# Low parts of the keys' weights on one engine, and another place for the conformer's norm, in a hybrid attention, Hyena and conformer layer

## The chip, the cores and the metric

The kernel runs on one core of a Trainium2 chip. The core has engines with a queue of instructions each: TensorE (PE in the profile; PEld are its weight loads), VectorE (DVE), ScalarE (ACT), GpSimd (POOL) and SyncE (SP), which here only issues transfers; 16 DMA engines move the data. An engine works through its queue in order. The metric is the device time of one execution in microseconds (us); several timed runs are taken, and one more execution is recorded by the hardware profiler.

## The reference

One layer over 512 latent tokens of width 1024, arranged as 8 rows of 64, and 256 context tokens:

```
h  = modulate(rmsnorm(x), sh1, sc1);   hc = modulate(rmsnorm(ctx), csh1, csc1)
q, k, v, hy_in, cf_in = split(h @ w_in);   kc, vc = hc @ w_in[:, keys and values]
attn = softmax over (an 8 x 16 window of latents, and all context) in 8 heads of 64
hy   = two gated long convolutions of hy_in
y    = depthwise_conv31(a * sigmoid(g)) + b,          a, g = split(cf_in)   # 512 x 256
cf   = silu((y - mean(y)) * rsqrt(var(y) + eps) * ln_g + ln_b)              # over the 256 channels
x    = x + g1 * (concat(attn, hy, cf) @ w_out)
x    = x + g2 * expert_choice_moe(modulate(rmsnorm(x), sh2, sc2))           # 16 experts, 64 tokens each
out  = rmsnorm(x)
```

All inputs and the output are fp32. The last line of the conformer, from the mean to the silu, is the norm over channels of which the change speaks.

## The kernel before

**Exact products from two halves.** The projections run on TensorE in a rounded fp32 format. To keep precision each operand is split in a high part (a copy in the rounded format, on ACT, L515) and a low part (the rest, a subtraction, L516). A product is then three matmuls that add up in one PSUM bank (mm3, L547): high by high (L548), high by low (L549), low by high (L550). split (L510) treats a weight buffer of 128 x 2048 in four pieces of 512 columns. The table DVE_LO (L491) lists, for each weight buffer, the pieces whose subtraction goes to VectorE; the others go to GpSimd. The keys' weights are two buffers: ('k', 0) with the first half of the 1024 input channels and ('k', 1) with the second; each has two pieces in the table.

**Stages.** The Hyena, conformer, query and value parts of the projection come first, woven together by an order string (L823). Beside them runs conv_cf (L585), the 31-tap convolution: two channel tiles, 31 dependent steps on VectorE each (L587, L590), into the tiles yc. The values' projection ends with the context's values, ctx_v, whose second result is copied from PSUM by VectorE (L105, vc). The small products of the modulation, adaln(2), come about there too; their results are read from PSUM by VectorE at L459 (a bank of tag T) and L486 (a bank of tag Y).

Then `finish(ln_cf())` (L826) issues the whole norm. ln_cf (L595) is a generator of two steps. Step one: two matmuls with ones give the channel mean (L598), VectorE subtracts it (L601), ACT squares into two tiles sq (L603). Step two: 16 small matmuls sum the squares per token (L609), twelve tiny VectorE operations form the reciprocal root (rsqrt_mean, L144 to L154), a diagonal tile dg is filled (L614), a matmul spreads it (L616), VectorE multiplies (L618), ACT applies the silu (L619), and mix_store writes the result as high part (ACT, L561) and low part (VectorE, L562) into the tiles mixh and mixl of the output projection.

Behind it in the program come the splits of the two keys' weight buffers (L855), fetch_bias(0) (two transfers of the position bias into tiles g, issued by POOL, L841), build_tm(0) (a memset at L845 and six POOL subtractions from g, L849, three for each g), and fetch_bias(1), two more g.

Then the keys (L872 to L894): for each half u of the input channels, first the products for the context (tiles pC, four of 128 x 256, L884 by mm3), then those for the latents (pP, four of 128 x 512), 48 matmuls each. The context's banks are taken from the tags T and Y in turn (tiles 0 and 2 from T, 1 and 3 from Y), and all are held from u = 0 to the copies behind the products of u = 1 (L887, L889). The third bank user of the norm, like its first two (all psY, "pL"), is of tag Y as well.

Attention follows. On TensorE its order is written out (L1100): a score step S (L932), the output projection's first part x0 for one block of tokens (out_part, L903, four channel tiles: two of the Hyena, two of the conformer), a score step, a transposition T, and so on. build_tm(1) and fetch_bias(2) stand ahead of it (L1097). The experts come last: 384 transfers of 1 MB for their weights.

**Order and buffers.** Outside the stretches with a written order, a list scheduler in the compiler sets each engine's queue: it takes what is ready by its own estimate of times, the earliest in the program first. Tiles with the same tag share a fixed number of buffers: PSUM has tags A (4 banks), T (2) and Y (2); the big weight tiles share 24 buffers (U); the tiles named g, sq, dg, xo and some others (L98) share two buffers of the pool early. A tile's buffer is released when its last reader is done. The helpers used, free and pump (L61 to L82) count big buffers in program order and issue the next weight transfers while the count is low enough.

Of the kernel before, what the change touches and what calls it, by code (L numbers as in the profile page):

```python
# [50 lines left out]
def hybrid_kernel(ctx: ExitStack, tc: tile.TileContext, a, out: bass.AP):  # L51
# [13 lines left out]
    def U(name, dt=FT):  # L65
        used[0] += 1
        assert used[0] <= NU, name
        return big.tile([128, 2048], dt, name=name, tag="U")
# [11 lines left out]
    def free_only(k=1):  # L80
        used[0] -= k
# [7 lines left out]
    def psY(name="psY"):  # L89
        return psum.tile([128, 512], FT, name=name, tag="Y", bufs=2)  # L90

    def W(name="w", dt=FT):
        if name in ("g", "aff2", "lists", "od", "sn", "u", "xo", "sig", "sq", "dg", "arg", ):
            return early.tile([128, 512], dt, name=name, tag="w", bufs=2)
        return work.tile([128, 512], dt, name=name, tag="w")
# [4 lines left out]
    def copy(out_, in_):  # L100
        alt[0] ^= 1
        if alt[0]:
            nc.scalar.activation(out_, in_, AF.Copy)  # L103
        else:
            nc.vector.tensor_copy(out_, in_)  # L105
# [30 lines left out]
    def small_t(name, n, dt=FT, bufs=2):  # L136
        return work.tile([128, n], dt, name=name, tag=name, bufs=bufs)

    def rsqrt_mean(dst, ss, n, scale=1.0 / D):

        v = small_t("rv", n)
        t = small_t("rt", n)
        y = small_t("ry", n, I32)
        nc.vector.tensor_scalar(v, ss, scale, EPS, op0=OP.mult, op1=OP.add)  # L144
        nc.vector.tensor_scalar(y, v.bitcast(I32), -0.5, 1597463007.0, op0=OP.mult, op1=OP.add)
        nc.vector.tensor_scalar(v, v, -0.5, None, op0=OP.mult)
        yf = y.bitcast(FT)
        for i in range(3):
            if n == 1:
                nc.vector.scalar_tensor_tensor(t, yf, v, yf, op0=OP.mult, op1=OP.mult)  # L150
            else:
                nc.vector.tensor_mul(t, yf, yf)
                nc.vector.tensor_mul(t, t, v)
            nc.vector.scalar_tensor_tensor(dst if i == 2 else yf, t, 1.5, yf, op0=OP.add, op1=OP.mult)  # L154
# [11 lines left out]
    def take(key):  # L166
        while key not in ready:
            assert loads and used[0] < NU, key
            go = loads.popleft()
            if go is not None:  # L170
                go()
        return ready.pop(key)
# [315 lines left out]

    ADA_KEEP = [7, 4, 2, 0]
    KEEP = {'hy1': 8, 'hy0': 7, 'cf': 10, 'q': 8, 'v': 7}  # L490
    DVE_LO = {('q', 0): (0, 2), ('q', 1): (1, 3), ('k', 1): (0, 1), ('k', 0): (2, 3), ('cf', 1): (0, 1), ('hy0', 1): (2, 3), ('cf', 0): (1, 3), ('hy0', 0): (0, 2)}  # L491
    ADA = [(4, 0), (4, 4), (2, 8), (2, 10)]

    def modulate_split(src, n, v, name, pool="01010101"):
# [15 lines left out]
    def split(raw, keep, dve=()):  # L510
        hi = U("wh", FR)
        lo = U("wl", FR)
        for i in range(4):
            s = slice(i * 512, (i + 1) * 512)
            nc.scalar.activation(hi[:, s], raw[:, s], AF.Copy)  # L515
            (nc.vector if i in dve else nc.gpsimd).tensor_sub(lo[:, s], raw[:, s], hi[:, s].bitcast(FT))  # L516
        free(1, keep)
        return hi, lo
# [5 lines left out]
    def next_split():  # L524
        c, u = splits.popleft()
        presplit[c, u] = split(take(("win", c, u)), KEEP[c], DVE_LO.get((c, u), ()))

# [19 lines left out]
    def mm3(ps, l, r, start, stop):  # L547
        mm(ps, l[0], r[0], start=start, stop=False)  # L548
        mm(ps, l[0], r[1], start=False, stop=False)  # L549
        return mm(ps, l[1], r[0], start=False, stop=stop)  # L550
# [7 lines left out]
    def mix_store(i, k, src):  # L558

        h = cr(v512(mixh[i])[:, k])  # L560
        nc.scalar.activation(h, tr(src), AF.Copy)  # L561
        nc.vector.tensor_sub(cr(v512(mixl[i])[:, k]), tr(src), h.bitcast(FT))  # L562
# [32 lines left out]
    def ln_cf():  # L595
        ps = psY("pL")
        for i in range(2):
            mm(ps, ones, yc[i], start=(i == 0), stop=(i == 1))  # L598
        sq = []
        for i in range(2):  # L600
            nc.vector.tensor_sub(yc[i], yc[i], ps)  # L601
            sq.append(W("sq"))
            nc.scalar.activation(sq[i], yc[i], AF.Square)  # L603
        yield

        ps = psY("pL")
        for c in range(4):
            for i in range(2):
                mm(ps[:, c:c + 1], sq[i][:, 128 * c:128 * c + 128], one256, start=(i == 0), stop=(i == 1))  # L609
        rs = small_t("rsl", 4, bufs=1)  # L610
        rsqrt_mean(rs, ps[:, 0:4], 4, 1.0)
        dg = W("dg")
        for c in range(4):
            nc.vector.tensor_scalar(dg[:, 128 * c:128 * c + 128], ident, rs[:, c:c + 1], 256.0, op0=OP.mult, op1=OP.mult)  # L614
        ps = psY("pL")
        mm(ps, ones, dg, start=True, stop=True)  # L616
        for i in range(2):
            nc.vector.tensor_mul(yc[i], yc[i], ps)  # L618
            nc.scalar.activation(yc[i], yc[i], AF.Silu,  # L619
                                 scale=p1[:, P1["lg"].start + i:P1["lg"].start + i + 1],  # L620
                                 bias=p1[:, P1["lb"].start + i:P1["lb"].start + i + 1])
            mix_store(1, 2 + i, yc[i])
        free_only(1)
        yield
# [145 lines left out]
    def finish(*gens):  # L770
        for g in gens:
            for _ in g:
                pass
# [46 lines left out]
    with ExitStack() as ordered:  # L820
# [2 lines left out]
        for w in "......s.............h............hh.......m...hm..h...h....m..m..h...h..h...h...m....hh..........h.m...mm..hh...n.h.h....h..c....m..xcnh..n..hh..m....c....c..n..c.sxn.m....c.c.c........c..c..x..c.....cc.....c........cccccccccccc":  # L823
            next(side[w], None)
        finish(side["."], *[side[w] for w in "hmncx"])
    finish(ln_cf())  # L826
    vblk = lambda c: vv[:, c // 16] if c % 16 == 0 else vo[:, c // 16]


# [6 lines left out]
    def fetch_bias(hp):  # L836
        for s in range(2):
            rb[hp, s] = g = W("g")[:, 0:8 * RPBW]
            src = bass.AP(tensor=rp.tensor, offset=rp.offset + (2 * hp + s) * 15 * RPBW,
                          ap=[[1, 16], [RPBW, 8], [1, 7 * RPBW + 48]])  # L840
            nc.gpsimd.dma_start(g[:, 0:7 * RPBW + 48], src)  # L841
# [12 lines left out]
    for u in range(2):  # L854
        parts.append([t.rearrange("p (k n) -> p k n", n=512) for t in split(take(("win", "k", u)), 2, DVE_LO.get(("k", u), ()))])  # L855
    fetch_bias(0)
# [6 lines left out]
    def load_wo(n, u, keep):  # L863
        w = take(("wo", n, u))
        if u == 0:
            for k in range(4):
                nc.vector.tensor_mul(v512(w)[:, k], v512(w)[:, k], g1bc[:, n * 512:(n + 1) * 512])
        hi, lo = split(w, keep)
        wov[n, u] = (v512(hi), v512(lo))
# [5 lines left out]
    for u in range(2):  # L875
        hi, lo = parts[u]
        if u:
            KK.extend([U("KK") for _ in range(2)])
        for ctx_ in (True, False):
            for m in range(4):  # L880
                s = slice(m * 128, (m + 1) * 128)
                for k in range(4):
                    kg = 4 * u + k
                    mm3((psc if ctx_ else pss)[m], (hi[:, k, s], lo[:, k, s]),  # L884
                        (ch(kg), cl(kg)) if ctx_ else (hh(kg), hl(kg)), kg == 0, kg == 7)
                if u and ctx_:
                    copy(kat(m)[:, 512:768], psc[m])  # L887
                elif u:
                    copy(kat(m)[:, 0:512], pss[m])  # L889
            if u and ctx_:  # L890
                free_only(2)
                load_wo(0, 1, 2)
        if u == 0:
            free_only(2)  # L894
# [578 lines left out]
```

## Time and profile before

| | us |
|---|---|
| median of 3 timed runs | 1320.08 (1317.94 to 1324.70) |
| profiled execution | 1325.77 |
| its span, first to last instruction | 1324.0 |
| busy: PE, DVE, ACT, POOL | 1247.9, 512.2, 223.7, 155.2 |
| mean granted TensorE clock, share of 2.4 GHz | 0.988 |
| DMA over the span | 345 GB/s |

Stages in the profiled execution, in us from the start of the span: projections to 212.6; keys to 258.8; attention and output projection to about 360; routing to 388; experts to the end. All times below are on that scale. In the rows, `a<-b,c` says that tile a is written from b and c, `xN` that N instructions are merged, and a bracket gives the idle time of the engine before them with what ended it. Matmul ends are modelled, so starts are safer than durations.

### The profile page before, as it was taken

Reading aid. Unit: us, or ns where it says so; the run is one execution under the profiler, and the core shown is the slowest. Engines: PE = TensorE matmul, PEld = TensorE weight load, DVE = VectorE, ACT = ScalarE, POOL = GpSimd, SP = SyncE. Lnnn points to the kernel's source line nnn. Section 1 sums busy time; section 2 is a strip of 40 time slices with the busy share of each in tenths; the row PEclk is TensorE's granted clock in tenths of the full one; section 3 lists DMA queues with packets and bytes.
Section 4 is the critical chain, followed back from the end, with each engine's and each line's share of the span. In section 5 each row is a group of like instructions: output and inputs, shape, how many; then the busy total and the mean of one; then the engine's idle time right before and its main releaser. Section 6 shows DMA issues by size and latency. Waiting matters only on the chain.

```text
span 1324.0 us, 14793 instructions
## 1 busy us (share of the span) xinstructions
PE 1247.9 (94%) x5916; PEld 566.1 (43%) x5916; DVE 512.2 (39%) x1034; ACT 223.7 (17%) x480; POOL 155.2 (12%) x166
## 2 busy tenths in 40 slices
PE   5899988999889999999999999999999999999996
PEld 2577667866634333333333333333333333333332
DVE  6878998788570121222212123121211212121232
ACT  3542232345410010101101011010101001010111
POOL 1343443556210000000000000000000000000000
PEclk9999998999989999999999999999999999999999
DMA  9944026532488999999999999999999999999997
GB/s 349 382 170 187 21 68 180 206 110 96 148 362 355 419 420 419 420 419 419 420 420 419 420 419 420 420 419 420 419 420 420 419 420 419 420 420 420 419 419 296
DMA packets 72979, 457.99 MB, mean 346 GB/s; under 512 B 7364, under 2 KB 9228, under 8 KB 21710
## 3 DMA queue, kind: packets, MB, share of 16 engines
q1 hardware_dynamic: 71662, 453.64, 84.4%
q0 software_dynamic: 912, 3.06, 0.8%
q8 instruction: 46, 0.75, 0.2%
q10 hardware_dynamic: 336, 0.35, 0.1%
q14 instruction: 23, 0.19, 0.0%
HBM read 453.87 MB, written 2.36 MB: 345 GB/s over the span
## 4 chain that ended last, share of the span: by engine, by line
PE 50%; DMA 33%; DVE 13%; issue 2%; ACT 2%; POOL 0%; POOLq 0%; SPq 0%; ACTq 0%; DVEq 0%
DMA ld<-in_w_dram 32%; PE pa L1309 18%; PE py L1349 8%; DVE glu L590 4%; PE pZ L1202 3%; PE pG L1182 2%; PE pa L1310 1%; PE pP L550 1%; PE pP L549 1%; PE pP L548 1%; PE pX L548 1%; PE pS L932 1%; DMA out_dram<-acc 1%; PE pO L963 1%; PE pX L549 1%
## 5 line engine op out<-in xcount | busy, mean ns | idle before, releaser
L1310 PE MATMUL pa<-ld,xh 128*64 128x512 f32 x1024 | 465.0, 599 | 13.3 <-DMA ld<-in_w_dram 13.3
L1309 PE MATMUL pa<-ld,xh 128*64 128x512 f32 x1024 | 467.2, 599 | 0.2 <-DVE xh L1062 0.2
L1349 PE MATMUL py<-ld,xh 128*64 128x512 f32 x1024 | 224.8, 596 | 1.0 <-DMA ld<-in_w_dram 1.0
L1309 PEld LDWEIGHTS pa<-ld,xh 128*64 128x64 f32 x1024 | 132.2, 137 | 215.2 <-issue 207.0
L1205 DVE TENSOR_TENSOR acc<-acc,pZ 128x512 f32<-128x512 f32 x112 | 73.2, 685 | 286.3 <-PE pZ L1202 285.8
L1310 PEld LDWEIGHTS pa<-ld,xh 128*64 128x64 f32 x1024 | 132.7, 137 | 87.9 <-issue 56.6
L1349 PEld LDWEIGHTS py<-ld,xh 128*64 128x64 f32 x1024 | 72.2, 138 | 141.9 <-issue 136.6
L1377 POOL DMA_INDIRECT out_dram<-yg,rwA x1 | 1.1, 1112 | 931.2 <-DVE yg L1376 931.2
L1060 ACT ACTIVATE xh<-pT,B,A 128x64 f32<-128x64 f32 (+1 forms) x60 | 24.4, 406 | 447.8 <-PE pT L1190 337.1
L1353 DVE SCALAR_TENSOR_TENSOR yg<-py,rwA,g1bc 128x512 f32<-128x512 f32 x16 | 12.0, 751 | 211.5 <-PE py L1349 211.5
L1202 PE MATMUL pZ<-yg,oh 64*128 64x512 f32 x240 | 83.2, 640 | 3.0 <-DVE acc L1205 2.3
L516 POOL TENSOR_TENSOR wl<-ld,wh 128x512 fp32r<-128x512 f32 x44 | 65.0, 1506 | 79.2 <-ACT wh L515 60.5
L548 PE MATMUL pP<-hh,wh 128*128 128x512 f32 x144 | 58.3, 406 | 1.2 <-ACT hh L505 1.2
L549 PE MATMUL pP<-hl,wh 128*128 128x512 f32 x144 | 57.0, 397 | 1.5 <-DVE hl L507 1.5
L550 PE MATMUL pP<-hh,wl 128*128 128x512 f32 x144 | 56.4, 398 | 1.1 <-DVE wl L516 1.1
L590 DVE SCALAR_TENSOR_TENSOR glu<-glu,p 128x512 f32<-128x512 f32 x60 | 55.3, 922 | 1.2
L1336 PE MATMUL pT<-c,au 128*128 128x128 f32 x256 | 48.1, 316 | 6.2 <-DVE xh L1339 2.2
L1182 PE MATMUL pG<-ld,ohg 128*64 128x512 f32 x224 | 52.5, 592 | 0.0
L103 ACT ACTIVATE xg<-pG 128x512 f32<-128x512 f32 x7 | 4.2, 598 | 275.0 <-PE pG L1182 275.0
L1062 DVE TENSOR_SCALAR xh<-pT,A,B 128x64 f32<-128x64 f32 (+1 forms) x60 | 20.6, 344 | 76.1 <-ACT xh L1060 28.5
L1202 PEld LDWEIGHTS pZ<-yg,oh 64*128 64x128 f32 x240 | 22.1, 184 | 63.2 <-issue 37.3
L1336 PEld LDWEIGHTS pT<-c,au 128*128 128x128 f32 x256 | 36.1, 209 | 26.9 <-DVE acc L1205 12.5
(342 smaller groups left out, 1349.8 us busy)
## 6 DMA issues: line engine op xcount, KB each, us to landing
ld<-in_w_dram SPq DMA_DIRECT2D x384, 1024.0 KB, 19.9
ld<-in_w_mod_dram SPq DMA_DIRECT2D x24, 1024.0 KB, 14.7
ld<-in_w_in_dram SPq DMA_DIRECT2D x11, 1024.0 KB, 7.5
ld<-in_w_out_dram SPq DMA_DIRECT2D x4, 1024.0 KB, 11.9
ld<-in_x_dram SPq DMA_DIRECT2D x2, 1024.0 KB, 12.0
ld<-in_x_dram SPq DMA_DIRECT2D x4, 512.0 KB, 6.6
out_dram<-acc SPq DMA_DIRECT2D x4, 512.0 KB, 16.8
g<-in_rpb_dram POOLq DMA_DIRECT2D x8, 244.5 KB, 4.6
```

The lines of the kernel that those rows point to most:

```text
L516: (nc.vector if i in dve else nc.gpsimd).tensor_sub(lo[:, s], raw[:, s], hi[:, s].bitcast(FT))
L548: mm(ps, l[0], r[0], start=start, stop=False)
L549: mm(ps, l[0], r[1], start=False, stop=False)
L550: return mm(ps, l[1], r[0], start=False, stop=stop)
L590: nc.vector.scalar_tensor_tensor(yc[i], glt[i][:, j:j + 512], cw[:, i, j:j + 1], yc[i], op0=OP.mult, op1=OP.add)
L1182: mm(pg[64 * h:64 * h + 64], g[:, 64 * b:64 * b + 64], xblk(b)[:, 512 * h:512 * h + 512], start=(b == 0), stop=(b == 3))
L1202: mm(ps[h], oh[pr, 128 * c:128 * c + 128], yg[pr], start=True, stop=True)
L1205: nc.vector.tensor_add(ablk(c)[:, s], (ablk if e else xblk)(c)[:, s], ps[h])
L1309: mm(pa[f][0:64], xT[:, k, cs], w1[:, s], start=(k == 0), stop=(k == 7))
L1310: mm(pa[f][64:128], xT[:, k, cs], w3[:, s], start=(k == 0), stop=(k == 7))
L1336: nc.tensor.transpose(p[:, i * 128:(i + 1) * 128], au[f][:, c:c + 255:2], ident)
L1349: mm(py[64 * h:64 * h + 64], hT[:, f], w2[:, i * 1024 + 512 * h:i * 1024 + 512 * h + 512], start=(f == 0), stop=(f == 15))
```

## The change

Two things. The entries of the keys' weights leave the table, so that all eight low pieces are subtracted by GpSimd. And the norm is no longer issued whole ahead of the keys: the generator is kept, and one step of it is issued behind the latents' products of tile 2 in the first half of the input channels, the other behind those of tile 3.

```
-    DVE_LO = {('q', 0): (0, 2), ('q', 1): (1, 3), ('k', 1): (0, 1), ('k', 0): (2, 3), ('cf', 1): (0, 1), ...}
+    DVE_LO = {('q', 0): (0, 2), ('q', 1): (1, 3), ('cf', 1): (0, 1), ...}
...
-    finish(ln_cf())
+    norm = ln_cf()
...
                 if u and ctx_:
                     copy(kat(m)[:, 512:768], psc[m])
                 elif u:
                     copy(kat(m)[:, 0:512], pss[m])
+                elif not ctx_ and m > 1:
+                    next(norm)
```

In program order the norm now stands behind the splits of the keys' weights, fetch_bias(0), build_tm(0), fetch_bias(1), all context products of the first half and the latent products of its tiles 0 to 2 (3 for the second step).

## Rows read from the trace of the kernel before

**Rows 1.** The page's part 4: the chain that ended last, share by engine.
```profile
PE 50%; DMA 33%; DVE 13%; issue 2%; ACT 2%; POOL 0%; POOLq 0%; SPq 0%; ACTq 0%; DVEq 0%
```

**Rows 2.** Stretches: length, busy us of PE, PEld, DVE, ACT, POOL, clock, DMA.
```profile
215.00:220.70 5.70, 1.81 (x10) 1.20 (x8) 5.49 (x8) 0.00 (x0) 0.35 (x1) 0.89 1.02 227
220.70:226.30 5.60, 5.60 (x15) 4.08 (x16) 4.66 (x11) 2.06 (x3) 0.00 (x0) 0.50 1.03 361
...
258.80:330.00 71.20, 67.57 (x462) 46.64 (x464) 59.67 (x138) 35.76 (x90) 43.12 (x45) 1.00 0.35 129
470.00:1324.00 854.00, 821.92 (x3618) 294.51 (x3614) 185.43 (x382) 72.82 (x175) 1.11 (x1) 0.99 1.00 415
```

**Rows 3.** PE's instructions in order of time: start, us, what.
```profile
220.68 2.07 PE L598 MATMUL pL<-glu,stat 128*128 128x512 f32 x2 [3.89 <-DVE glu L590]
```

**Rows 4.** The chain that ended last, pieces in order: start, us, what.
```profile
209.16 1.68 DVE glu L590
...
216.72 0.76 DVE glu L590
...
226.62 0.12 PE pC L550
...
228.18 0.23 PE pP L550
...
229.80 1.46 PE pL L609 x14
...
258.80 1.06 PE pS L932 x4
```

**Rows 5.** Instructions on tile pC in a stretch; columns PE, PEld, DVE, ACT.
```profile
214.00:238.20 24.20, 5.28 (x24) 4.40 (x25) 0.68 (x1) 0.00 (x0) 0.86 0.57 160
```

**Rows 6.** POOL's instructions in order of time.
```profile
156.12 1.68 POOL L685 TENSOR_TENSOR t<-xo,KE 128x512 f32<-128x512 f32 x1 [0.63 <-DVE t L687]
...
194.67 0.77 POOL L899 DMA_DIRECT2D vodd<-v  x1 [8.62 <-ACT v L103]
...
208.56 3.43 POOL L516 TENSOR_TENSOR wl<-ld,wh 128x512 fp32r<-128x512 f32 x2
...
231.90 0.56 POOL L841 DMA_DIRECT2D g<-in_rpb_dram  x1 [16.55 <-PE pL L609]
...
248.01 5.03 POOL L516 TENSOR_TENSOR wl<-ld,wh 128x512 fp32r<-128x512 f32 x4
258.63 0.31 POOL L845 MEMSET tm<- 128x256 f32 x1 [5.60 <-PE pP L549]
258.90 4.62 POOL L849 TENSOR_TENSOR tm<-c,g 128x256 f32<-128x256 f32 x6
```

**Rows 7.** VectorE's instructions in order of time.
```profile
220.54 0.68 DVE L105 COPY vc<-pC 128x512 f32<-128x512 f32 x1
...
231.29 0.16 DVE L144 TENSOR_SCALAR rv<-pL 128x4 f32<-128x4 f32 x1 [5.90 <-PE pL L609]
...
233.61 0.88 DVE L614 TENSOR_SCALAR dg<-c,rsl 128x128 f32<-128x128 f32 x4
239.78 1.29 DVE L618 TENSOR_TENSOR glu<-glu,pL 128x512 f32<-128x512 f32 x2 [5.29 <-PE pL L616]
...
246.29 1.61 DVE L562 TENSOR_TENSOR mixl<-glu,mixh 128x512 fp32r<-128x512 f32 x1
...
248.16 5.76 DVE L562 TENSOR_TENSOR mixl<-glu,mixh 128x512 fp32r<-128x512 f32 x1
```

**Rows 8.** ACT's instructions in order of time.
```profile
224.23 1.23 ACT L603 ACTIVATE sq<-glu 128x512 f32<-128x512 f32 x2 [12.11 <-DVE glu L601]
...
240.50 1.52 ACT L619 ACTIVATE glu<-glu,p 128x512 f32<-128x512 f32 x2 [13.74 <-DVE glu L618]
241.93 1.14 ACT L561 ACTIVATE mixh<-glu 128x512 fp32r<-128x512 f32 x1
...
300.52 2.18 ACT L515 ACTIVATE wh<-ld 128x512 fp32r<-128x512 f32 x4
```

More of the change, by code (lines that the diff above doesn't have):

```diff
@@ L490, in hybrid_kernel @@
     KEEP = {'hy1': 8, 'hy0': 7, 'cf': 10, 'q': 8, 'v': 7}
-    DVE_LO = {('q', 0): (0, 2), ('q', 1): (1, 3), ('k', 1): (0, 1), ('k', 0): (2, 3), ('cf', 1): (0, 1), ('hy0', 1): (2, 3), ('cf', 0): (1, 3), ('hy0', 0): (0, 2)}
+    DVE_LO = {('q', 0): (0, 2), ('q', 1): (1, 3), ('cf', 1): (0, 1), ('hy0', 1): (2, 3), ('cf', 0): (1, 3), ('hy0', 0): (0, 2)}
     ADA = [(4, 0), (4, 4), (2, 8), (2, 10)]
```

## The prediction

> **What bounds the kernel now.** I read the chain that ended last first: half of it is matmul time and a third is transfers of expert weights [rows 1]. From 470 us on the DMA engines are busy all the time [rows 2], so the experts run at the rate of their weights, and these start when buffers come free at the end of attention: whatever moves that end moves the end of the kernel by as much. Ahead of it, in the keys' projection and the attention, TensorE works nearly without a gap (67.57 of 71.20 us between 258.80 and 330) [rows 2]. So I read the change from TensorE's queue between the values' projection and the first outputs of attention.
>
> There the stretches [rows 2] and the instructions in order of time [rows 3] show one hole. TensorE idles 3.89 us for the second product of the channel mean (L598), which waits for the last step of the 31-tap convolution on VectorE, and then works 5.6 us at a granted clock of 0.50, the lower of its two levels (1.2 GHz): 2.8 us more. Then it is busy until the first scores at 258.80, which I call T [rows 4]. Work between: 96 products on the context at 0.12 us and 96 on the latent tokens at 0.23 [rows 4], 33.3 us in all.
>
> The last thing to see is who gets a buffer. POOL issues the transfers into vodd at 194.67, but those into g, which stand ahead of them in the program, only at 231.90, when L609 has read sq [rows 6]. The two buffers of that tag were last read by POOL's L685 at 156.12 (xo) [rows 6], so they lay empty for some 66 us and g was not given one, because sq, sq and dg come first in the program. PSUM says the same: of the first half's 48 context products only 24 run before 238.2 [rows 5], those of tiles 0 and 2; tiles 1 and 3 need the banks of tag Y and wait until the norm's third bank (L616) has been handed out. I take it that buffers of one tag go out in program order.
>
> **Low parts on POOL.** VectorE loses four subtractions, POOL gains four; on VectorE they lay behind the convolution, so this alone saves no step of TensorE. A convolution step takes 0.76 us alone and 1.68 beside a POOL piece [rows 4]. Before, two pairs of pieces ran beside it (the first, 208.56, took 3.43) [rows 6]; now eight follow each other, to about 222, and four more steps are slow: 4 x 0.9 = 3.6 us. The convolution ends at 224.2 instead of 220.6. Bounds: nothing (no step hit), and 4 x 1.68 = 6.7. The pieces are in time themselves: those of the first half end near 215.4, the others near 222, ahead of their products.
>
> The Trainium skill (SBUF — State Buffer, "SBUF: two separate sides") holds the port pair that VectorE and GpSimd share to be an exclusive lock on which the loser fully blocks, and counts a VectorE operation with two SBUF inputs in. By that each added piece would cost its own length, 5.03 / 4 = 1.26 us [rows 6], 5.0 in all, and the forecast would be 1.4 us higher; the pair measured here, 1.68 against 0.76 + 1.26, is shorter than that, so I keep the row.
>
> **TensorE at the start of the keys.** The norm's L598 no longer stands there. But VectorE is one queue, and behind the convolution wait the copy of vc (0.68) [rows 7], which frees the accumulator of the fourth key tile, and the short L459 and L486, which free a bank each of tags T and Y for context tiles 2 and 3. So the wait stays, for another reader. TensorE gets some 2.5 us of products in, then stands until 224.2 + 0.7 + 0.1 = 225.0, where it had gone on at 220.68. After that before took 258.80 - 220.68 = 38.1 us; now 0.9 us of products are already done, both L598 come behind (one more, 1.0, half of the 2.07 at the low clock [rows 3]), and L609 (1.6 by its 14 records of 1.46 [rows 4]) and L616 (1.0, the same shape) leave this stretch: 35.6. The slow clock I keep at 2.8. The scores start at 260.6, **1.8 us later**. Bounds: 249.5, if the compiler finds 11 us of products that need nothing of VectorE (a rival), and 262 by the convolution's upper end.
>
> **The norm.** It now stands behind the context products of the first half and behind fetch_bias(0), build_tm(0) and fetch_bias(1). Two things hold it. Its first bank comes after those of context tiles 1 and 3, which are read only in the second half; so L598 runs about 10 us ahead of T, in no one's way. And sq comes after the four g of fetch_bias(0) and (1), so both sq wait until build_tm(1) has read the third and fourth. That one waits for the end of the keys: before, its memset was issued at 258.63, released by the last L549 [rows 6], as a weight buffer had to come free. In the new program the convolution's own buffer is also still held, and nothing lets it start sooner.
>
> From T: six subtractions on POOL end at T+4.7 (258.90 + 4.62) [rows 6]; second square 0.6 [rows 8]; L609 1.7; the reciprocal root from 231.29 to 233.61, 2.3; dg 0.9 [rows 7]; L616 1.0, 2.0 at the low clock, I take 1.2: T+11.4. From the product with the mean's root (239.78) to the end of the second high part is 243.07 + 1.1, so 4.4 [rows 7, 8]; the first low part (1.61) follows the first high part, the second follows it: 6.6 to its end: T+18.0 [rows 7]. TensorE's order is written out there: one score step, then the output product x0 over four channel tiles, of which the last two are the conformer's. It does 1.06 + 6 x 0.23 = 2.4 us and stops; x0 ends at T+18.3 where it ended at T+3.8: **14.5 us**, and 2.8 for the lower clock after so long a hole. Attention cannot make it up: each later score stands behind x0 in the same queue.
>
> Bounds of this part: 0 if the buffers come otherwise (rivals), and up to 2 x (5.76 - 1.61) = 8.3 more if POOL works beside both low parts, as beside one before [rows 7].
>
> **At nothing.** One buffer fewer is free when weights of w_out are fetched, so its third block is issued during the second half; it is first split at 300.52 [rows 8], 40 us later. If that cover went, the split would wait for one transfer. g's first transfers and build_tm(0) come earlier, on a POOL that then idles.
>
> **Sum.** 1.8 + 14.5 + 2.8 = 19.1 us over the profiled execution, which took 1325.77 (span 1324.0). The timed runs lie lower, median 1320.08 (1317.94 to 1324.70); on that it makes **1339 us**, 1.4% slower.
>
> **Rivals.**
> *Buffers go to whoever is ready (chance 0.10).* Then the norm runs among the first half's products, the hole of 3.89 and the 2.8 of slow clock go, and nothing waits behind T: 1320.1 - 6.7 = 1313. For it: nothing but that the products named are enough to fill the hole. Against: g and tiles 1 and 3 [rows 5, 6]. It decides when sq is written before build_tm(1).
> *The keys lose their hole, the norm is still late (0.18).* Tiles 0 and 1 on the context and 0 to 2 on the latents need nothing behind the convolution: 24 x 0.12 + 36 x 0.23 = 11.2 us, from 214.1 to 225.3, just enough. T would be 214.1 + 33.3 + 2.1 = 249.5, 9.3 earlier, and 17.3 later follow: 1328. Against: context tiles 2 and 3 come ahead in the program and their banks look free as soon as the convolution is taken to be over.
> *Only the banks hold the norm (0.05).* It then starts about 10 us ahead of T and x0 waits some 3 us: 1320.1 + 1.8 + 3 = 1325.
> *The chain behind T is longer (0.10).* Both low parts beside POOL, or behind the products of w_out with the gate: 1339 + 8.3 = 1348.
> My forecast keeps 0.57, with 1334 to 1344 as its own range.
>
> **How the numbers follow.** Measurements of this kernel cannot tell changes under about 0.5%, 6.6 us, from none: faster is below 1313.5, slower above 1326.7. The first rival gives 0.10 for faster, though it sits on that line; the third, with a little more, 0.06 for the same; the rest, 0.84, is slower. A range of 1325 to 1348 holds the forecast, the second rival, and parts of the third and fourth.
>
> **What would show it.** In the new profile: eight pieces of wl on POOL in a row and eight convolution steps near 1.68; g issued before 200 us; a wait of TensorE of about 8 us for VectorE near 217; L598 past 240, L603 after L849 of build_tm(1); and, after the first scores, a hole of 12 to 16 us ahead of pX that ends with L561 or L562. I am wrong if L603 comes before the last key product, or if TensorE has no hole after the first scores.

## The result

The changed kernel takes 1340.34 us (median of 4 runs, 1337.92 to 1341.89) where the kernel before, timed beside it, takes 1322.39 (4 runs, 1317.94 to 1325.99): 1.0129 times as long, interval 1.0102 to 1.0156. The forecast was 1339 us. A second series of the same kernel ("changed, once more" below) gave 1340.34 again and 1.0124 [1.0097, 1.0151].

The two profiled executions lie less far apart: 1339.2 us (span 1336.5) against 1325.77, so 13.4. Single executions of the kernel before range from 1317.23 to 1328.15 over 34 runs, so one pair of profiles cannot say what a few us are. The mean granted clock sorts these 34: the 16 at 0.992 or more took 1317.23 to 1322.32, the 18 at 0.990 or less 1323.03 to 1328.15, and the profiled one (0.988) is of the longer kind, 3.4 us above the median beside it, while the changed kernel's lies 1.1 below its own. Part of this scatter lies outside the change: the products on q's weights, of which nothing was edited, begin at 172.51 before and at 171.49 after, and in the experiments between 171.04 and 174.52. I therefore measure each kernel from that row to three marks: the end of the convolution (the copy of vc behind it), the first scores T, and the second score step, which stands behind the first block of x0. TensorE of the kernel before, in order of time:

```profile
172.51 1.20 PE L548 MATMUL pP<-wh,hh 128*128 128x512 f32 x4 [1.50 <-ACT wh L515]
...
258.73 1.13 PE L932 MATMUL pS<-KK,Q 64*128 64x512 f32 x4
...
262.75 1.13 PE L932 MATMUL pS<-KK,Q 64*128 64x512 f32 x4
...
268.60 1.13 PE L932 MATMUL pS<-KK,Q 64*128 64x512 f32 x4
```

The same of the changed kernel, whose lines behind the norm's new place have numbers two higher (they answer [rows 3]):

```profile
171.49 0.73 PE L548 MATMUL pP<-wh,hh 128*128 128x512 f32 x2 [1.53 <-ACT wh L515]
...
222.47 0.58 PE L548 MATMUL pC<-hch,wh 128*128 128x256 f32 x1 [4.24 <-DVE mT L459]
...
243.01 1.88 PE L598 MATMUL pL<-glu,stat 128*128 128x512 f32 x4
...
255.73 1.13 PE L934 MATMUL pS<-KK,Q 64*128 64x512 f32 x4
...
271.67 0.80 PE L548 MATMUL pX<-wh,mixh 128*128 128x512 f32 x1 [3.28 <-ACT mixh L561]
...
274.77 2.01 PE L934 MATMUL pS<-KK,Q 64*128 64x512 f32 x4
...
281.87 1.13 PE L934 MATMUL pS<-KK,Q 64*128 64x512 f32 x4
```

The scores start 84.24 us behind the common row instead of 86.22: 2.0 earlier. Then the second score step comes 19.04 us behind the first instead of 4.02. That one stretch is the loss: 15.0 us more. Over all, the second score step lies 103.28 behind the common row instead of 90.24, 13.0 later. The clock is not back by then: it stays at 0.50 from 274.77 to 276 and has a mean of 0.85 from 276 to 278, and the third score step follows after 7.10 us instead of 5.85. With that 1.25 the third score step lies 14.3 later.

The chain that ended last names the stretch piece by piece. It can be followed no further back than to build_tm(1), and its first pieces are those of the norm (the longest ones, the answer to [rows 4]):

```profile
256.73 3.89 POOL tm L849 x5
260.64 0.64 ACT sq L603
261.33 1.74 PE pL L609 x14
265.38 0.89 DVE dg L614 x4
266.31 2.09 PE pL L616 x2
268.43 0.70 DVE glu L618
269.15 1.52 ACT glu L619 x2
270.67 0.96 ACT mixh L561
271.67 0.80 PE pX L548
```

Stretches of the changed kernel (columns as in [rows 2]): the start of the keys, the hole, what runs at the low clock behind it, the rest of the keys, from the first to the second score step, and the experts:

```profile
214.71:218.23 3.52, 3.52 (x21) 2.78 (x20) 3.45 (x3) 0.00 (x0) 3.52 (x4) 1.00 1.03 229
218.23:222.47 4.24, 0.00 (x1) 0.01 (x1) 4.10 (x6) 0.00 (x0) 4.24 (x5) 0.94 1.02 238
222.47:225.00 2.53, 2.53 (x12) 2.53 (x13) 1.48 (x3) 0.00 (x0) 2.53 (x3) 0.50 0.73 270
225.00:255.73 30.73, 30.73 (x168) 26.05 (x167) 8.97 (x13) 5.32 (x9) 9.13 (x10) 0.99 0.59 222
255.73:274.77 19.04, 9.99 (x35) 5.44 (x34) 9.77 (x29) 8.70 (x12) 5.93 (x9) 0.69 0.28 82
...
470.00:1336.00 866.00, 835.38 (x3674) 298.48 (x3672) 189.12 (x390) 72.82 (x175) 1.12 (x1) 0.99 1.00 415
```

TensorE works 9.99 of the 19.04 us, part of it at the low clock. The last line reads as in [rows 2]: the experts still run at the rate of their weights, so what attention lost is not made up.

POOL, VectorE and ACT of the changed kernel, the answers to [rows 6 to 8]:

```profile
145.54 0.77 POOL L841 DMA_DIRECT2D g<-in_rpb_dram  x1
...
209.20 8.49 POOL L516 TENSOR_TENSOR wl<-ld,wh 128x512 fp32r<-128x512 f32 x5 [1.67 <-ACT wh L515]
217.63 0.30 POOL L845 MEMSET tm<- 128x256 f32 x1
217.90 5.91 POOL L849 TENSOR_TENSOR tm<-c,g 128x256 f32<-128x256 f32 x6
223.76 3.83 POOL L516 TENSOR_TENSOR wl<-ld,wh 128x512 fp32r<-128x512 f32 x3
...
255.69 0.31 POOL L845 MEMSET tm<- 128x256 f32 x1 [7.41 <-PE pP L549]
255.97 4.64 POOL L849 TENSOR_TENSOR tm<-c,g 128x256 f32<-128x256 f32 x6
```
```profile
206.63 15.10 DVE L590 SCALAR_TENSOR_TENSOR glu<-glu,p 128x512 f32<-128x512 f32 x12
221.65 0.68 DVE L105 COPY vc<-pC 128x512 f32<-128x512 f32 x1
222.25 0.16 DVE L459 COPY mT<-pT 128x16 f32<-128x16 f32 x1
...
271.65 2.05 DVE L562 TENSOR_TENSOR mixl<-glu,mixh 128x512 fp32r<-128x512 f32 x2 [1.94 <-ACT mixh L561]
```
```profile
258.46 0.61 ACT L603 ACTIVATE sq<-glu 128x512 f32<-128x512 f32 x1
...
260.64 0.63 ACT L603 ACTIVATE sq<-glu 128x512 f32<-128x512 f32 x1 [0.87 <-POOL tm L849]
```

The reader is to see three things. g is fetched from 145.54 on instead of 231.90 [rows 6], and build_tm(0) runs beside the convolution. The second sq is released by build_tm(1) (0.87 <- POOL tm), more than 17 us behind L598. And TensorE's hole at the keys now ends with mT, which VectorE reads right behind the convolution.

### The profile page after: what moved, and what is told of

It reads as the page before. It is cut to its first block, busy times and chain, and to the rows that moved or that the text cites. A ratio compares the mean times of both kernels' runs of the same rounds, so it can differ in the third digit from the quotient of the medians.

```text
span 1336.5 us, 14785 instructions
## 1 busy us (share of the span) xinstructions
PE 1252.0 (94%) x5916; PEld 566.6 (42%) x5916; DVE 504.1 (38%) x1030; ACT 225.2 (17%) x481; POOL 164.4 (12%) x170
## 3 DMA queue, kind: packets, MB, share of 16 engines
q0 software_dynamic: 912, 3.06, 1.0%
## 4 chain that ended last, share of the span: by engine, by line
PE 42%; DMA 33%; DVE 3%; ACT 1%; issue 1%; POOL 0%; POOLq 0%; SPq 0%; ACTq 0%; DVEq 0%
DMA ld<-in_w_dram 31%; PE pa L1311 19%; PE py L1351 8%; PE pZ L1204 3%; PE pG L1184 2%; DMA out_dram<-acc 1%; PE pS L934 1%; PE pT L1338 1%; PE pO L965 1%; PE pX L548 1%; PE pX L550 1%; PE pX L549 1%; PE pT L954 1%; PE pT L1167 1%; DVE acc L1207 1%
## 5 line engine op out<-in xcount | busy, mean ns | idle before, releaser
L1312 PE MATMUL pa<-ld,xh 128*64 128x512 f32 x1024 | 465.1, 599 | 11.4 <-DMA ld<-in_w_dram 11.4
L516 POOL TENSOR_TENSOR wl<-ld,wh 128x512 fp32r<-128x512 f32 x48 | 71.7, 1523 | 89.6 <-ACT wh L515 86.2
L590 DVE SCALAR_TENSOR_TENSOR glu<-glu,p 128x512 f32<-128x512 f32 x60 | 56.4, 940 | 1.2
```

Source lines behind the costliest of these rows:

```text
L590: nc.vector.scalar_tensor_tensor(yc[i], glt[i][:, j:j + 512], cw[:, i, j:j + 1], yc[i], op0=OP.mult, op1=OP.add)
L1312: mm(pa[f][64:128], xT[:, k, cs], w3[:, s], start=(k == 0), stop=(k == 7))
```

## The experiments

Ratios are to the kernel before, timed beside each; the last three columns are the distances from the common row.

| kernel | median us | ratio, 95% interval | convolution ends | T | second scores |
|---|---|---|---|---|---|
| before (its first profile) | | 1 | 48.03 | 86.22 | 90.24 |
| changed (its first profile) | 1340.34 | 1.0129 [1.0102, 1.0156] | 50.16 | 84.24 | 103.28 |
| norm alone | 1336.84 | 1.0110 [1.0089, 1.0131] | 50.42 | 84.70 | 104.15 |
| low parts alone | 1329.56 | 1.0044 [1.0028, 1.0061] | 51.75 | 89.78 | 93.80 |
| own buffers | 1333.70 | 1.0074 [1.0056, 1.0092] | 50.83 | 87.78 | 98.48 |
| fetch behind | 1331.01 | 1.0059 [1.0037, 1.0080] | 50.87 | 87.72 | 98.27 |
| banks | 1330.71 | 1.0062 [1.0042, 1.0081] | 50.99 | 76.90 | 97.38 |
| buffers and banks | 1316.93 | 0.9953 [0.9933, 0.9973] | 50.19 | 81.18 | 85.20 |
| the same, low parts shared | 1323.41 | 0.9999 [0.9981, 1.0016] | 48.66 | 87.32 | 91.34 |
| shared, build_tm(0) later | 1323.99 | 1.0016 [0.9999, 1.0033] | 49.68 | 87.29 | 91.31 |
| buffers and banks, build_tm(0) later | 1315.91 | 0.9950 [0.9932, 0.9967] | 51.76 | 81.16 | 85.18 |
| before, banks alone | 1325.03 | 1.0007 [0.9985, 1.0029] | 48.06 | 86.04 | 90.06 |
| changed, once more | 1340.34 | 1.0124 [1.0097, 1.0151] | 50.30 | 84.54 | 103.58 |
| buffers and banks, second half shared | 1316.25 | 0.9940 [0.9917, 0.9964] | 50.45 | 79.57 | 83.59 |

The last column less 90.24 gives the sign and most of the size of each ratio that is clear of 1: -6.7 us where 0.9940 makes -7.9, +8.2 where 1.0074 makes +9.8, +13.3 where 1.0124 makes +16.4. The change acts inside this stretch. What is over is up to 4 us, and most for the changed kernel. Where TensorE has a hole ahead of x0, some 1.3 us of it are the low clock behind the second score step: to the third it takes 7.20 us with own buffers and 7.16 in the changed kernel's second profile, against 5.86 with buffers and banks. The rest stays unlocated.

### The two parts apart

Norm alone, on the changed kernel:
```
-    DVE_LO = {('q', 0): (0, 2), ('q', 1): (1, 3), ('cf', 1): (0, 1), ...}
+    DVE_LO = {('q', 0): (0, 2), ('q', 1): (1, 3), ('k', 1): (0, 1), ('k', 0): (2, 3), ('cf', 1): (0, 1), ...}
```


> The norm's move alone; the keys' low parts are shared between VectorE and POOL as before. Theory (the norm's move is nearly all of the loss): the hole ahead of the first output products stays, 13 to 17 us, with the low clock after it, and the first scores come near 255 us; the time is that of the changed kernel within 5 us, ratio to before 1.009 to 1.016. Rival (POOL's eight pieces are needed for the loss, since they delay the whole chain that frees g): ratio below 1.005.

Low parts alone, on the kernel before: the reverse edit.

> The low parts on POOL alone; the norm stands ahead of the keys as before. Theory as on record: the convolution ends up to 3.6 us later and TensorE's wait for it grows by as much, 0 to +3.6 us, ratio 1.000 to 1.003; by the profile of the changed kernel, in which the convolution ended 1.0 us later, nearer to +1. No hole behind the first scores. Rival (each added piece costs VectorE its own length, 1.26 us, and weights of the second half come late for TensorE): +5 us and more, ratio over 1.004.

Measured: 1.0110 and 1.0044. The norm's move makes the hole behind T (19.45 us from T to the second scores) and most of the loss, as the theory had it. The low parts cost 5.8 us by the ratio, more than the 0 to 3.6 expected and as much as the rival's 5 and more. But the profile shows the theory's mechanism: the stretch grew by 3.6, the convolution ended 3.7 later, and TensorE waits for no low part of POOL. What the ratio has over 3.6 stays unlocated. TensorE's wait in it, and the convolution beside POOL (a group of one line: count, shortest/median/longest ns, first and last start):

```profile
224.52 2.07 PE L598 MATMUL pL<-glu,stat 128*128 128x512 f32 x2 [7.44 <-DVE glu L590]
```
```profile
L590 DVE SCALAR_TENSOR_TENSOR glu<-glu,p x9: 752/1642/1677, 208.7 to 221.3; 128x512 f32<-128x512 f32 x9
```

Eight of these nine steps take 1.63 to 1.68 us, one for each of POOL's eight pieces; the ninth runs alone. In the kernel with the norm alone, POOL does two pieces, then build_tm(0), then two pieces beside the convolution; its steps in the middle stretch, the POOL instructions there, and what TensorE then waits for:

```profile
L590 DVE SCALAR_TENSOR_TENSOR glu<-glu,p x7: 1131/1151/1672, 211.4 to 219.0; 128x512 f32<-128x512 f32 x7
```
```profile
L849 POOL TENSOR_TENSOR tm<-c,g x6: 971/1224/1227, 212.7 to 218.4; 128x256 f32<-128x256 f32 x6
```
```profile
224.77 0.58 PE L550 MATMUL pC<-hch,wl 128*128 128x256 f32 x1 [5.16 <-DVE wl L516]
```

So the early build_tm(0) is not free: beside each subtraction (1.22) a convolution step takes 1.15 instead of 0.75. And with the low parts shared, TensorE waits 5.16 us for one that stands behind the convolution on VectorE. The two parts therefore do not add: 13.9 and 3.6 us in the stretch alone, 13.0 and 13.3 together.

### What holds the norm

Own buffers, on the changed kernel (`early` has two buffers for all names in the list):
```
-        if name in ("g", "aff2", "lists", "od", "sn", "u", "xo", "sig", "sq", "dg", "arg", ):
+        if name in ("g", "aff2", "lists", "od", "sn", "u", "xo", "sig", "arg", ):
```


> The changed kernel, but sq and dg take buffers of the general pool and no longer share two with g. Theory (buffers of one tag go out in program order, so g held sq): the second L598 stays near 244 us, since its bank still comes behind context tiles 1 and 3, but both squares follow it at once, before build_tm(1), L609 and L616 come ahead of the first scores, and the hole of some 15 us ahead of the output product goes, with its 2.8 us of low clock: 1318 to 1324, ratio 0.996 to 1.002. Rival (the banks alone would hold the norm long enough): the output product still waits 3 us or more, ratio 1.002 to 1.006. Rival (something else than g holds sq): the hole stays, ratio over 1.009.

Fetch behind, on the changed kernel:
```
     build_tm(0)
-    fetch_bias(1)
...
+    fetch_bias(1)
     free(6, 4)
```


> The changed kernel with fetch_bias(1) written behind the keys' loop, so that its two g come after sq and dg in the program; no buffer is added. Theory (buffers of one tag go out in program order): both squares follow L598 at once, as with own buffers: L603 near 249, ahead of build_tm(1); the hole shrinks to some 5 us and the time is that of the run with own buffers, 1.005 to 1.009. Rival (what counts is not the order but that three kinds share two buffers): squares late, 1.010 to 1.014.

Both squares now follow L598 at once; ACT of own buffers, and of fetch behind:

```profile
248.66 1.23 ACT L603 ACTIVATE sq<-glu 128x512 f32<-128x512 f32 x2 [1.35 <-DVE glu L601]
```
```profile
246.87 1.23 ACT L603 ACTIVATE sq<-glu 128x512 f32<-128x512 f32 x2 [1.35 <-DVE glu L601]
```

Nothing but the order of allocation differs between fetch behind and the changed kernel, and it does what more buffers do: g held sq because it comes first in the program. But own buffers missed the expected 1318 to 1324 and passed the rival's 1.002 to 1.006 too. There the time from T to the second scores falls from 19.04 to 10.70 us, not to 4, and T itself comes 3.5 us later than in the changed kernel: L609 now runs ahead of it, and TensorE waits 6.59 us for mT at the start of the keys instead of 4.24. L598 still comes at 246.03 for want of a bank, and then the queues decide. dg is complete at 259.10, but in TensorE's queue L616 stands behind the first scores and six products of x0 and begins at 263.13; VectorE has the first scores' work ahead of L618, which runs at 264.94; and x0 waits 4.02 us for mixh.

Banks, on the changed kernel: two context accumulators to a bank, so that one bank of T and one of Y stay free; the norm uses one bank for its three results:
```
-        ps = psY("pL")
...
-        ps = psY("pL")
...
-    psc = [(psT, psY)[m % 2]("pC")[:, 0:256] for m in range(4)]
+    pcb = [psT("pC"), psY("pC")]
+    psc = [pcb[m // 2][:, 256 * (m % 2):256 * (m % 2) + 256] for m in range(4)]
...
-                        (ch(kg), cl(kg)) if ctx_ else (hh(kg), hl(kg)), kg == 0, kg == 7)
+                        (ch(kg), cl(kg)) if ctx_ else (hh(kg), hl(kg)), kg == 0 and not (ctx_ and m % 2), kg == 7 and not (ctx_ and m % 2 == 0))
                 if u and ctx_:
-                    copy(kat(m)[:, 512:768], psc[m])
+                    for j in (m - 1, m) if m % 2 else ():
+                        copy(kat(j)[:, 512:768], psc[j])
```


> The changed kernel, but the four context accumulators of the keys lie two to a bank (each bank opened by one start, both halves copied out behind the second), and the norm uses one bank for its three results; sq and dg share buffers with g as in the changed kernel. Theory (g holds sq): L598 runs some 15 us earlier, near 225, the wait of 4.2 us at the start of the keys shrinks below 1 us as no context tile waits for a bank of L459 or L486, but the squares still wait for build_tm(1) and the hole behind the first scores stays: first scores near 251 to 253, time 1333 to 1340, ratio 1.007 to 1.014. Rival (the banks hold the norm): the hole goes, ratio 0.993 to 1.002.

TensorE in order of time, then ACT (the norm's later lines and build_tm have numbers one or two lower here):

```profile
228.32 1.88 PE L598 MATMUL pL<-glu,stat 128*128 128x512 f32 x4
...
249.55 1.13 PE L934 MATMUL pS<-KK,Q 64*128 64x512 f32 x4
...
255.15 3.15 PE L608 MATMUL pL<-stat,sq 128*128 128x1 f32 x14 [1.82 <-ACT sq L603]
...
270.03 2.05 PE L934 MATMUL pS<-KK,Q 64*128 64x512 f32 x4
```
```profile
254.47 0.63 ACT L603 ACTIVATE sq<-glu 128x512 f32<-128x512 f32 x1 [0.87 <-POOL tm L847]
```

L598 runs 16 us earlier from the common row and it does not help: the second sq still waits for build_tm(1). The ratio, 1.0062, is a little below the 1.007 to 1.014 of the theory. The hole at the start of the keys is gone: T is 9.3 us earlier than before, which is the 3.89 and the 2.8 of the low clock plus 2.6 for the L609 and L616 that left this stretch.

Buffers and banks: both edits.

> Own buffers for sq and dg and two context accumulators to a bank, together, on the changed kernel: nothing but the convolution is left to hold the norm. Theory (g's buffers and the banks are the two things that delayed it): L598 near 229, L609 near 234, L616 near 240, all among the keys' products; first scores near 252 (249.55 with the banks alone, plus 2.6 for L609 and L616 coming ahead of them), no hole behind them, so 6 to 7 us less than before: 1315 to 1320, ratio 0.993 to 0.997. Rival (a third holder, VectorE's or ScalarE's own order): a hole of 3 us or more stays ahead of the output product, ratio over 1.000.

```profile
228.57 1.88 PE L598 MATMUL pL<-glu,stat 128*128 128x512 f32 x4
...
252.48 1.13 PE L934 MATMUL pS<-KK,Q 64*128 64x512 f32 x4
...
256.50 1.13 PE L934 MATMUL pS<-KK,Q 64*128 64x512 f32 x4
```
```profile
215.00:235.00 20.00, 20.00 (x115) 17.05 (x115) 9.93 (x12) 1.23 (x2) 13.50 (x14) 1.00 0.60 147
```

TensorE is busy all of 215 to 235 at the full clock, the norm lies among the keys' products, and 4.02 us pass from T to the second scores. At 0.9953 this version beats both kernels. Two holders explain the delay, each enough to keep a hole, and with both gone no third shows.

Before, banks alone: the second edit on the kernel before, where the norm's code stays.

> The kernel before with two context accumulators to a bank, and nothing else: the norm stands ahead of the keys and the low parts are shared. Theory (TensorE's hole of 3.89 us is set by the place that L598 has in TensorE's queue, which stands ahead of products that then need no bank): the compiler may put more products ahead of L598, as in the runs with the banks; then the hole and its 2.8 us of low clock go, first scores near 252 to 254, ratio 0.994 to 0.998. Rival (L598 keeps its place): no difference, 0.999 to 1.001.

1.0007, and TensorE again waits 3.90 us for L590: L598 keeps its place in the queue. A free bank gains nothing while the waiting product stands first.

### The low parts again

The same, low parts shared: DVE_LO as in the kernel before, on buffers and banks.

> The last one with the keys' low parts shared between VectorE and POOL as before. Theory: with products enough to fill TensorE until the convolution ends, what the low parts cost the convolution no longer shows; within 2 us of the last one, ratio 0.992 to 0.998. Rival (the low parts still cost their 5.8 us measured alone): 4 to 6 us faster than the last one.

Both expectations were wrong: it is slower, 0.9999 against 0.9953. TensorE, and its stretch from 215 to 235:

```profile
224.99 0.48 PE L550 MATMUL pC<-hch,wl 128*128 128x256 f32 x1 [2.29 <-DVE wl L516]
...
226.67 0.58 PE L550 MATMUL pC<-hch,wl 128*128 128x256 f32 x1 [0.77 <-DVE wl L516]
```
```profile
215.00:235.00 20.00, 16.94 (x93) 15.24 (x92) 13.05 (x16) 0.73 (x2) 12.10 (x12) 0.83 0.71 183
```

Two holes of 3.06 us together, and a mean clock of 0.83, make T 6.1 us later (87.32 against 81.18 from the common row); the holes are half of it.

Shared, build_tm(0) later, and buffers and banks, build_tm(0) later: on each of the two versions just shown,
```
     fetch_bias(0)
-    build_tm(0)
-    fetch_bias(1)
...
         if u == 0:
             free_only(2)
+            build_tm(0)
+            fetch_bias(1)
```


> The run with own buffers, shared banks and shared low parts, in which build_tm(0) and fetch_bias(1) now stand behind the keys' first half instead of ahead of it. Theory (each POOL instruction makes the one convolution step beside it longer, 0.9 us for a low part and 0.4 for a subtraction of build_tm; TensorE then waits for low parts that stand behind the convolution on VectorE): the six subtractions leave the convolution, it ends 2.3 us earlier, TensorE's waits of 2.29 and 0.77 us for wl shrink to under 1.5 together; 1318 to 1322, ratio 0.996 to 0.999. Rival (the wait for wl is not the convolution's doing): no difference, 0.999 to 1.001.

> The run with own buffers and shared banks, low parts on POOL alone, with build_tm(0) and fetch_bias(1) behind the keys' first half. Theory: eight low parts now follow each other on POOL and the convolution has eight steps near 1.65, so it ends some 2 us later than with build_tm(0) in between; but nothing that TensorE does before 228 waits for it, so no difference to that run: ratio 0.993 to 0.998. Rival (the convolution's end still sets the norm and with it the scores): 2 us slower than that run.

The first says nothing on its question: POOL did four pieces and then build_tm(0) beside the convolution all the same, and neither the wait for wl (2.79 and 0.16 us, before it 2.29 and 0.77) nor the time changed beyond the intervals. In the second the edit took: eight pieces in a row, a convolution that ends 1.6 us later from the common row, and the same time, 0.9950. There the convolution's end no longer counts.

Second half shared: buffers and banks with `('k', 1): (0, 1)` alone back in the table.

> The run with own buffers and shared banks, in which only the second half's low parts are shared with VectorE again, those of the first half stay on POOL. Theory (with all shared, TensorE waited 3.06 us and lost some 3 us of clock, because two low parts of the first half stood behind the convolution on VectorE; those of the second half are not read before 231 us): no such wait, the time of the run with all on POOL, ratio 0.993 to 0.998. Rival (any low part on VectorE costs, whichever half): 1320 to 1324, ratio 0.998 to 1.001.

0.9940, with no wait in the keys. So only the first half's two pieces on VectorE cost, by standing behind the convolution. The intervals of this and the other two versions near 0.995 overlap.

Changed, once more:

> The changed kernel once more, unedited, for a second profile and more times. In the first pair of profiles the stretch from the first product on q's weights to the second score step grew by 13.0 us, while the medians lay 18.0 apart. If the profiles are right: 1335 to 1338, ratio 1.009 to 1.012. If the medians are: 1339 to 1343, ratio 1.012 to 1.015, and the second profile shows a longer stretch than 103.3 us, as its convolution runs beside POOL's pieces from the first on.

The medians repeat, in the range of the second expectation. But the second profile's stretch is 103.58, hardly longer, its convolution runs beside five pieces and build_tm(0) as in the first, and its own execution (1336.87) is the shortest of its five. What the other executions add stays open.

## Why the prediction was right, and where not

**The norm, 14.5 us and 2.8 of clock: right.** T to the second scores grew by 15.0 us, and to the third, when the clock is back, by 16.3; 17.3 were foretold. By its steps: POOL's subtractions ended at T+4.9 (foretold 4.7), L616's start at the low clock put its end near T+12.7 (11.4), the low parts ended at T+18.0 (18.0), x0 near T+19.0 (18.3). Both low parts together took 2.05 us, where 1.61 had been taken for each [rows 7]: POOL was idle, which won back the loss at L616. That g holds sq until build_tm(1) is shown twice, by more buffers and by another order alone. The banks were taken for harmless, "in no one's way"; they are so only while sq is later still. With sq free they keep 6.7 us of the 15.0.

**TensorE at the start of the keys, +1.8 us: wrong in sign.** T came 2.0 earlier. The mechanism was right (the wait stays, for mT's bank), but it is 4.24 us, not about 8, and two terms were mis-sized. The convolution ended 2.1 us later, not 3.6. And behind the hole 33.3 us passed to T, not 35.6: TensorE had 3.5 us of products done, not 2.5, and the low clock cost some 1.4 (half of the 2.53 us at 0.50, and a little behind them), not 2.8. Two sums of the prediction do not come out of their own terms: 96 products at 0.12 and 96 at 0.23 make 33.6 us, not 33.3, and with the convolution's upper end (220.6 + 6.7 = 227.3) the bound for T is 263.7, not 262. Neither moves the forecast.

**Low parts on POOL, 3.6 us: right by themselves, not in company.** Alone they made eight slow steps and moved the convolution's end by 3.7. In the changed kernel build_tm(0), which stood under "at nothing" on a POOL "that then idles", came between the fifth and sixth piece, beside the convolution: five steps near 1.66 and three near 1.13. The Trainium skill (SBUF — State Buffer, "SBUF: two separate sides") says that the loser of the shared ports fully blocks for the other's whole instruction; by that the four added pieces would have cost the 5.0 us of the prediction's estimate. Low parts alone show 3.7. The trace decides for the smaller figure: a step and a piece take turns, but the pair takes 1.65 to 1.75 us, not 0.76 + 1.26.

**What the prediction did not see.** With the norm behind, shared low parts would have been worse: the first products that TensorE lacks are then those on VectorE's two pieces of the first half. Moving the low parts to POOL costs 5.8 us on the kernel before and saves 6.1 once the norm is free (0.9999 against 0.9953).

**The sum.** 19.1 us were foretold from the rows of the profiled execution (1325.77) and put on a median of 1320.08; the profiles show 13.4, the medians 18.0 and 16.6. That 1339 lies so near to 1340.34 is in part luck: the terms are 3.8 too high for the start of the keys and 1.0 for the norm, and against that the kernel before, timed again, took 1322.39 instead of 1320.08, and the medians hold 3.7 us that do not show up to the third score step.

**Rivals.** "Buffers go to whoever is ready" fell with sq behind build_tm(1); that the keys lose their hole fell with the 4.24 us; the longer chain behind T fell with low parts that ended at T+18.0, beside an idle POOL. "Only the banks" is what own buffers leave, at +9.8 us rather than +5.

## What to carry to other kernels

Where work is moved in a program whose buffers go out in program order, list for each of its tiles who is allocated ahead of it in the same tag and when that one is read for the last time: two such holders, in SBUF and PSUM, turned a move meant for a gap into a stall, and freeing either alone brought back about half. Before an operation is shared with another engine, ask what stands ahead of it in that engine's queue; the same four subtractions cost 5.8 us in one order of the program and saved 6.1 in the other. Compare stretches from an unedited common row, since executions differ ahead of it by more than many effects.

## What was not expected of the hardware

Beside the convolution VectorE and POOL took strict turns: each POOL subtraction made exactly one convolution step longer, 1.63 to 1.68 us beside a low part, 1.13 to 1.15 beside a subtraction of build_tm, 0.75 alone, and POOL's own were longer too (1.72 for 1.26, 1.22 for 0.77). It is not so everywhere: in the kernel before, one low part of the norm on VectorE took 5.76 us beside four pieces of POOL, and these took only 1.26 each [rows 6, 7]; alone it takes 1.02. And in the version with buffers, banks and shared low parts the granted clock, 1.00 up to the end of the hole of 2.29 us, was 0.54 from 225.0 to 226.5 and 0.50 from there to 231, with the second hole of 0.77 us in it; that cost as much again as the holes.
